# Loading, scaling and transposing a scan's B, C and D once per layer instead of once per quarter of its groups

## The chip, the cores and the metric

The kernel runs on one core of one Trainium2 chip. The metric is the device time of one execution in microseconds (us), the median over several runs. In the views of the profile PE is TensorE (its matmuls), PEld its weight loads, DVE is VectorE, ACT is ScalarE, POOL is GpSimd and SP is SyncE. ACTq stands for a DMA that ACT issues: it takes up ACT's own instruction stream.

## What is computed

One inference step of a two-layer trunk on 512 latent tokens and 128 context tokens, width 1024, fp32. Each layer: a modulated RMS norm, one input projection whose columns feed three mixers (a state-space scan, latent attention, a gated chunk mixer), a merge and an output projection; then a second norm and a convolutional feed-forward block (FFN). The change touches the parameters of the scan alone:

```python
def ssm_direction(u, h0, a_re, a_im, b_re, b_im, c_re, c_im, log_dt, reverse):
    A = lax.complex(a_re, a_im)            # 16 groups, 64 states
    Bm = lax.complex(b_re, b_im)           # (16, 64, 16 channels)
    Cm = lax.complex(c_re, c_im)           # (16, 16, 64)
    a_bar = jnp.exp(A * jnp.exp(log_dt)[:, None])
    b_bar = ((a_bar - 1.0) / A)[..., None] * Bm
    bu = jnp.einsum('gpc,blgc->blgp', b_bar, u)
    ...
    _, h = lax.associative_scan(_scan_combine, (a, bu), axis=1, reverse=reverse)
    return jnp.einsum('gcp,blgp->blgc', Cm, h).real, h_final
y = y_forward + y_backward + ssm_d * u
```

Both directions, both layers. B and C depend on the layer and the direction, not on the tokens.

## The kernel before

The tokens lie transposed in SBUF, with the channels on the partitions. Layer 0 opens with 16 loads of `w_mod` (512 KB each, on SP's queue) for the modulation, and then normalises the tokens in two halves, `norm_apply` L347: per slice of 128 channels DVE forms `nt` (L353), ACT casts it to `hh` (L357), and DVE takes the rest `hl` (L358). PE's projections need both. The weights of the input projection come through SP too and are split by ACT (`wth`, L117) and DVE (`wtl`, L118).

The scan runs in blocks of 8 tokens, so that almost all of its work is matmuls against tables: `WEd` (into a block's states), `Qd` (out of them), `Wd` (the taps inside a block) and `Td` (the rotations from block to block). `ssm_tables` (L530) makes the first three for a quarter of the groups, four of the 16, as two pairs on the two halves of the partitions, and writes them to DRAM. `ssm_load` (L683) brings them back for `ssm_quarter`. Per quarter it

- loads B in eight pieces (L547), C in eight (L551) and D in four (L626), all issued by ACT;
- transposes C on PE, and ACT copies it to `CT` (L557);
- scales B by `f = (a_bar - 1) / A` to `bb`: 12 operations of 128x32 (L91 to L96);
- and for each direction raises `bb` by the powers of a_bar (`G`, six operations of 128x256), transposes that on PE (`we`, L147) and writes `WEd`; does the same with C (`tm`, `Q`: four operations of 128x288 and four of 64x288, L607 to L611) and writes `Qd`; and last multiplies the two for the taps (PE, L632 to L635).

In layer 0 quarters 0, 1 and 2 are made by DVE, quarter 3 and the rotations (`ssm_rotations`, L648, whose fourth of four parts is the last) by POOL, all while the projection runs. The first load of the scans is `T` from `Td` (L692, on POOL's queue); its buffer has held quarter 3's `Q` before. Layer 1's four quarters are made by POOL during layer 0's FFN, one as each of the first four chunks of the FFN is written (`hooks` in `run`). `pre` is a pool open only in the opening.

The order of the instructions on each engine is not the program's: a scheduler with a model of time sorts them by priority and readiness, and each engine then works through its own list in that order.

Of the kernel before, what the change touches and what calls it, by code (L numbers as in the profile page):

```python
# [47 lines left out]
class Trunk:  # L48
# [480 lines left out]

    def ssm_tables(self, l, q, pool, E, tags={}, ps_of=None):  # L530
# [10 lines left out]
        B = t("B", [128, 2, 2, 2, 16])  # L541
        Cr = t("Cr", [128, 128])
        for d in range(2):
            for h in range(2):
                g = h * 8 + 2 * q
                for ri, nm in enumerate(("re", "im")):
                    nc.scalar.dma_start(  # L547
                        out=B[h * 64:(h + 1) * 64, ri, d],
                        in_=I["ssm_b_" + nm][l, d, g:g + 2].rearrange("g p c -> p g c"))
                    r = (ri * 2 + d) * 32  # L550
                    nc.scalar.dma_start(  # L551
                        out=Cr[r:r + 32, h * 64:(h + 1) * 64],
                        in_=I["ssm_c_" + nm][l, d, g:g + 2].rearrange("g c p -> (g c) p"))
        ps = ps_of("ct")
        self.tr(ps[:, :128], Cr)
        CT = t("CT", [128, 2, 2, 2, 16])
        nc.scalar.copy(CT.rearrange("p a b c d -> p (a b c d)"), ps[:, :128])  # L557
        bb = t("bb", [128, 2, 2, 2, 16])
        tm = [t(f"tm{i}", [128, 2 * 9 * 16]) for i in range(2)]
        for d in range(2):  # L560
            sh = [128, 2, 16]
            cs = slice(c0 + 8 * d, c0 + 8 * d + 2)
            self.complex_mul(E, bb[:, 0, d], bb[:, 1, d], B[:, 0, d], B[:, 1, d],
                             bc(self.f[:, 0, cs, None], sh), bc(self.f[:, 1, cs, None], sh),
                             [x[:, :32].rearrange("p (a b) -> p a b", b=16) for x in tm])
# [3 lines left out]
        for ri in range(2):  # L569
            for h in range(2):  # L570
                nc.scalar.copy(
                    bs[ri * 64:(ri + 1) * 64, :128].rearrange("p (d h n) -> p d h n", d=2, h=2)[:, :, h],
                    bb[h * 64:(h + 1) * 64, ri].rearrange("p d g c -> p d (g c)"))
        Qs = []
        for d in range(2):
# [6 lines left out]
            def v4(a, n):  # L582
# [7 lines left out]
                             bc(bb[:, 0, d][:, :, None, :], shp), bc(bb[:, 1, d][:, :, None, :], shp),  # L590
# [11 lines left out]
            c_re = bc(CT[:, 0, d][:, :, None, :], shp)  # L602
            c_im = bc(CT[:, 1, d][:, :, None, :], shp)
# [1152 lines left out]
```

## Time and profile before

| | |
|---|---|
| median of 3 runs | 1834.89 us (1831.66 to 1836.72) |
| the profiled execution's own time | 1831.83 us |
| its span, first to last instruction | 1830.0 us |
| mean granted TensorE clock | 0.961 |
| PE, DVE, ACT, POOL busy | 93%, 63%, 37%, 17% of the span |
| layer 0 up to the last matmul of the scan output's gate | 241.3 us |

The profile says which engine worked when, and for an engine that stood still, what released it. An engine's total says little here, since the stages differ: PE is the limit in the FFNs, and not in the opening of layer 0. The windows below are cut at events of the opening: 53.5 us is the first `nt` of the first half of the norm, 64.7 the end of its last `hl`, 68.7 and 94.7 the same of the second half, 147.4 the issue of the scans' first load, 241.3 the last matmul of the scan output's gate.

### The profile page before, as it was taken

What the parts mean: (1) busy time and instruction counts of PE and PEld (TensorE: products, weight loads), DVE (VectorE), ACT (ScalarE), POOL (GpSimd) and SP (SyncE); (2) the same over time, 40 slices, a digit from 0 to 9 for tenths busy, and PEclk for the clock granted to TensorE, in tenths of its full rate; (3) what the DMA queues carried; (4) which work ended last, traced back from release to release, by engine and by line L of the source; (5) the groups of instructions that cost most, each with busy time, mean ns of one, the idle gap of its engine ahead of it and who ended that gap; (6) DMA issues with size and microseconds to landing.
All of it is one profiled execution on the core that took longest, in us unless ns stands there. A gap on an engine that the chain in (4) does not pass through costs nothing.

```text
span 1830.0 us, 28203 instructions
## 1 busy us (share of the span) xinstructions
PE 1708.6 (93%) x10864; PEld 1499.7 (82%) x10864; DVE 1158.5 (63%) x2421; ACT 681.7 (37%) x1210; POOL 311.4 (17%) x738
## 2 busy tenths in 40 slices
PE   6869789998999999999999888999989999999998
PEld 2668644478889999999999785445989999999998
DVE  6887875667664546456566668475786464555554
ACT  4334444433442424224244355353344232332241
POOL 2886200000195060540000210000000000000000
PEclk8989799999999999999999888999989999999999
DMA  9265453301453523223122633430222131221221
GB/s 297 70 177 152 113 166 122 105 24 47 129 160 111 152 55 117 76 81 110 47 78 79 169 87 121 157 127 1 70 70 93 35 104 47 92 89 39 81 82 58
DMA packets 192998, 182.44 MB, mean 100 GB/s; under 512 B 33438, under 2 KB 153052, under 8 KB 192864
## 3 DMA queue, kind: packets, MB, share of 16 engines
q1 hardware_dynamic: 170160, 154.33, 27.5%
q0 software_dynamic: 8272, 23.87, 4.4%
q10 hardware_dynamic: 14432, 2.44, 0.7%
q8 instruction: 86, 1.41, 0.3%
q14 instruction: 48, 0.39, 0.1%
HBM read 161.94 MB, written 18.64 MB: 99 GB/s over the span
## 4 chain that ended last, share of the span: by engine, by line
PE 75%; DVE 10%; DMA 8%; ACT 4%; issue 2%; POOL 1%; ACTq 1%; DVEq 0%; POOLq 0%
PE up L141 11%; PE up L143 11%; PE up L142 10%; PE dn L142 5%; PE dn L143 5%; PE dn L141 5%; PE mod L261 3%; DMA raw<-w_mod 3%; PE o L1287 3%; PE wo L141 1%; PE wo L143 1%; PE wo L142 1%; DVE wlo L118 1%; DMA raw<-ffn_w_up 1%; PE s L1267 1%
## 5 line engine op out<-in xcount | busy, mean ns | idle before, releaser
L141 PE MATMUL up<-hh,whi 128*128 128x322 f32 x1408 | 436.8, 315 | 9.8 <-ACT hh L357 8.9
L142 PE MATMUL up<-hl,whi 128*128 128x322 f32 x1408 | 439.2, 313 | 1.8 <-DVE hl L358 1.8
L143 PE MATMUL up<-hh,wlo 128*128 128x322 f32 x1408 | 439.8, 314 | 0.0
L141 PEld LDWEIGHTS up<-hh,whi 128*128 128x128 f32 x1408 | 266.1, 190 | 21.8 <-issue 10.8
L142 PEld LDWEIGHTS up<-hl,whi 128*128 128x128 f32 x1408 | 268.3, 191 | 2.7 <-DVE hl L358 2.7
L143 PEld LDWEIGHTS up<-hh,wlo 128*128 128x128 f32 x1408 | 267.3, 190 | 1.0 <-issue 1.0
L118 DVE TENSOR_TENSOR wlo<-raw,whi 128x1024 fp32r<-128x1024 f32 (+1 forms) x116 | 147.4, 1272 | 155.2 <-ACT whi L117 146.5
L142 PE MATMUL dn<-glo,dh 128*128 128x322 f32 (+1 forms) x704 | 217.7, 311 | 0.0
L143 PE MATMUL dn<-gh,dl 128*128 128x322 f32 (+1 forms) x704 | 217.4, 310 | 0.0
L141 PE MATMUL dn<-gh,dh 128*128 128x322 f32 (+1 forms) x704 | 208.9, 310 | 2.3 <-DVE xT L1501 1.5
L1501 DVE SCALAR_TENSOR_TENSOR xT<-dn,mod,xT 128x320 f32<-128x320 f32 (+2 forms) x288 | 112.1, 435 | 128.2 <-PE dn L143 128.1
L117 ACT CAST whi<-raw 128x1024 fp32r<-128x1024 f32 (+1 forms) x116 | 120.6, 1041 | 157.1 <-PE up L142 63.8
L1532 ACT ACTIVATE cv<-up,prm,cw 128x321 f32<-128x321 f32 x88 | 54.1, 619 | 259.0 <-PE up L143 255.0
L143 PEld LDWEIGHTS dn<-gh,dl 128*128 128x128 f32 x704 | 132.9, 189 | 0.0
L141 PEld LDWEIGHTS dn<-gh,dh 128*128 128x128 f32 x704 | 130.4, 189 | 2.8 <-DVE xT L1501 1.8
L142 PEld LDWEIGHTS dn<-glo,dh 128*128 128x128 f32 x704 | 132.7, 188 | 0.0
L261 PE MATMUL mod<-raw,sT 128*32 128x512 f32 x384 | 89.7, 642 | 21.7 <-DMA raw<-w_mod 19.8
L1533 DVE SCALAR_TENSOR_TENSOR cv<-up,cw,cv 128x320 f32<-128x320 f32 x88 | 48.3, 549 | 74.3 <-ACT cv L1532 74.1
L118 DVE TENSOR_TENSOR dl<-raw,dh 128x1024 fp32r<-128x1024 f32 x44 | 53.9, 1224 | 38.3 <-ACT dh L117 38.2
L1250 DVE TENSOR_REDUCE nml<-mx 128x1 f32<-128x640 f32 x64 | 51.1, 819 | 28.3 <-PE mx L1248 28.2
L117 ACT CAST dh<-raw 128x1024 fp32r<-128x1024 f32 x44 | 46.1, 1048 | 50.7 <-DMA raw<-ffn_w_down 44.5
L141 PE MATMUL wo<-yh,whi 128*128 128x322 f32 (+1 forms) x192 | 60.0, 318 | 1.7 <-ACT yh L117 0.9
(472 smaller groups left out, 3367.4 us busy)
## 6 DMA issues: line engine op xcount, KB each, us to landing
raw<-w_mod SPq DMA_DIRECT2D x96, 512.0 KB, 4.3
raw<-ffn_w_up SPq DMA_DIRECT2D x88, 512.0 KB, 3.9
raw<-ffn_w_down SPq DMA_DIRECT2D x44, 512.0 KB, 3.4
raw<-w_in SPq DMA_DIRECT2D x10, 512.0 KB, 5.0
we<-WEd POOLq DMA_DIRECT2D x8, 512.0 KB, 4.4
qt<-Qd POOLq DMA_DIRECT2D x8, 512.0 KB, 5.0
raw<-w_out SPq DMA_DIRECT2D x16, 256.0 KB, 4.8
raw<-w_out SPq DMA_DIRECT2D x8, 512.0 KB, 3.4
```

Source lines behind the costliest of these rows:

```text
L117: self.nc.scalar.copy(hi, raw)
L118: self.nc.vector.tensor_tensor(lo, raw, hi.bitcast(F32), op=OP.subtract)
L141: mm(ps, wh, xh, start=start, stop=False)
L142: mm(ps, wh, xl, start=False, stop=False)
L143: mm(ps, wl, xh, start=False, stop=stop)
L261: nc.tensor.matmul(ps[c:c + 32, :], self.sT[:, k, :], rv[:, j, :], start=k < 4, stop=k >= 4)
L1250: V.tensor_reduce(nm[:, tt:tt + 1], pb[:, :, :320], axis=AX.XY, op=OP.max, negate=True)
L1267: mm(ps, kh[i][:, kc_], qh[i], start=True, stop=False)
L1287: mm(pb[i * 64:(i + 1) * 64, 0], Vt[:, kt, 2 * p + i], Ps[i][kt], start=kt == 0, stop=kt == 4)
L1501: self.nc.vector.scalar_tensor_tensor(self.xT[:, m, a:b], po[:, a - lo:b - lo], self.modcol(l, gi, m, c), self.xT[:, m, a:b], op0=OP.mult, ...
L1532: A.activation(z[:, 0:321], po[:, 0:321], AF.Identity, bias=b, scale=c1)
L1533: V.scalar_tensor_tensor(z[:, 1:321], po[:, 0:320], c0, z[:, 1:321], op0=OP.mult, op1=OP.add)
```

## The change

A new `ssm_parts` runs once per layer. It loads all of B (eight pieces of 64x8x16), C (four) and D (four), transposes C in four pieces into one bank, which ACT copies out at once, and scales B with 12 operations of 128x128. The results stay in SBUF in `home`, and `ssm_tables` reads slices of it. Layer 0's runs on DVE while `w_mod` loads, and its `home` borrows the buffer of `yA`, the scan's output, which is allocated later for that. Layer 1's runs on POOL in the first hook of the FFN. Per layer ACT issues 16 such loads where it issued 80, with the same bytes; DVE in layer 0 has 12 operations of 128x128 in place of 36 of 128x32, and POOL 12 fewer of 128x32; the bigger operations on G and Q are the same.

```diff
@@ -527,6 +527,43 @@
+    def ssm_parts(self, l, pool, home, E, tags=("B", "Cr")):
+        nc, I = self.nc, self.I
+        B = pool.tile([128, 2, 2, 8, 16], F32, name=self.uid("B"), tag=tags[0], bufs=1)
+        Cr = pool.tile([128, 2, 2, 2, 64], F32, name=self.uid("Cr"), tag=tags[1], bufs=1)
+        self.bbt, self.cct = home[0], home[1]
+        for d in range(2):
+            for ri, nm in enumerate(("re", "im")):
+                for h in range(2):
+                    nc.scalar.dma_start(
+                        out=B[h * 64:(h + 1) * 64, ri, d],
+                        in_=I["ssm_b_" + nm][l, d, h * 8:h * 8 + 8].rearrange("g p c -> p g c"))
+                nc.scalar.dma_start(
+                    out=Cr[:, ri, d],
+                    in_=I["ssm_c_" + nm][l, d].rearrange("(h g) c p -> (g c) h p", h=2))
+        self.dct = self.cp.tile([128, 4], F32, name=f"dct{l}")
+        nc.gpsimd.memset(self.dct, 0.0)
+        for gq in range(4):
+            g = gq // 2 * 8 + gq % 2
+            nc.scalar.dma_start(
+                out=self.dct[gq * 32:gq * 32 + 16],
+                in_=bass.AP(tensor=I["ssm_d"].tensor, offset=I["ssm_d"][l, g * 16:].offset,
+                            ap=[[1, 16], [32, 4]]))
+        ps = self.pa("ct")
+        for i in range(4):
+            self.tr(ps[:, i * 128:(i + 1) * 128],
+                    Cr[:, i // 2, i % 2].rearrange("p h c -> p (h c)"))
+        nc.scalar.copy(self.cct.rearrange("p a b c d -> p (a b c d)"), ps)
+        tm = [pool.tile([128, 8, 16], F32, name=self.uid("bt"), tag=f"tm{i}", bufs=1)
+              for i in range(2)]
+        for d in range(2):
+            cs = slice(l * 16 + 8 * d, l * 16 + 8 * d + 8)
+            sh = [128, 8, 16]
+            self.complex_mul(E, self.bbt[:, 0, d], self.bbt[:, 1, d], B[:, 0, d], B[:, 1, d],
+                             bc(self.f[:, 0, cs, None], sh), bc(self.f[:, 1, cs, None], sh), tm)
+
...
-        B = t("B", [128, 2, 2, 2, 16])
-        Cr = t("Cr", [128, 128])
-        for d in range(2):
-            for h in range(2):
-                g = h * 8 + 2 * q
-                for ri, nm in enumerate(("re", "im")):
-                    nc.scalar.dma_start(
-                        out=B[h * 64:(h + 1) * 64, ri, d],
-                        in_=I["ssm_b_" + nm][l, d, g:g + 2].rearrange("g p c -> p g c"))
-                    r = (ri * 2 + d) * 32
-                    nc.scalar.dma_start(
-                        out=Cr[r:r + 32, h * 64:(h + 1) * 64],
-                        in_=I["ssm_c_" + nm][l, d, g:g + 2].rearrange("g c p -> (g c) p"))
-        ps = ps_of("ct")
-        self.tr(ps[:, :128], Cr)
-        CT = t("CT", [128, 2, 2, 2, 16])
-        nc.scalar.copy(CT.rearrange("p a b c d -> p (a b c d)"), ps[:, :128])
-        bb = t("bb", [128, 2, 2, 2, 16])
+        bb, CT, dall = self.bbt, self.cct, self.dct
+        g0 = slice(2 * q, 2 * q + 2)
         tm = [t(f"tm{i}", [128, 2 * 9 * 16]) for i in range(2)]
-        for d in range(2):
-            sh = [128, 2, 16]
-            cs = slice(c0 + 8 * d, c0 + 8 * d + 2)
-            self.complex_mul(E, bb[:, 0, d], bb[:, 1, d], B[:, 0, d], B[:, 1, d],
-                             bc(self.f[:, 0, cs, None], sh), bc(self.f[:, 1, cs, None], sh),
-                             [x[:, :32].rearrange("p (a b) -> p a b", b=16) for x in tm])
...
-                    bb[h * 64:(h + 1) * 64, ri].rearrange("p d g c -> p d (g c)"))
+                    bb[h * 64:(h + 1) * 64, ri, :, g0].rearrange("p d g c -> p d (g c)"))
...
-                             bc(bb[:, 0, d][:, :, None, :], shp), bc(bb[:, 1, d][:, :, None, :], shp),
+                             bc(bb[:, 0, d, g0][:, :, None, :], shp), bc(bb[:, 1, d, g0][:, :, None, :], shp),
...
-            c_re = bc(CT[:, 0, d][:, :, None, :], shp)
-            c_im = bc(CT[:, 1, d][:, :, None, :], shp)
+            c_re = bc(CT[:, 0, d, g0][:, :, None, :], shp)
+            c_im = bc(CT[:, 1, d, g0][:, :, None, :], shp)
...
-        dcol = t("dcol", [128, 1])
-        nc.gpsimd.memset(dcol, 0.0)
...
-                g = h * 8 + 2 * q + e
-                nc.scalar.dma_start(out=dcol[gq * 32:gq * 32 + 16],
-                                    in_=I["ssm_d"][l, g * 16:(g + 1) * 16].rearrange("(c o) -> c o", o=1))
...
-        V.scalar_tensor_tensor(W[:, 112:128], self.id16, dcol, W[:, 112:128],
+        V.scalar_tensor_tensor(W[:, 112:128], self.id16, dall[:, q:q + 1], W[:, 112:128],
...
-        yA = mt("yA", [128, 2, NT])
...
-                    "B": "we", "Cr": "qt", "CT": "tp", "bb": "bbg", "bs": "bsg"}
+                    "bs": "bsg"}
...
+            yA = mt("yA", [128, 2, NT])
...
             with tc.tile_pool(name="pre", bufs=1, side="right") as pre:
                 mix = self.begin_layer(0, self.mod_blocks(0, (2, 0, 3, 1), pre))
+                home = mix[2].tile([128, 2, 2, 2, 8, 16], F32, name="home", tag="yA", bufs=1)
+                self.ssm_parts(0, pre, (home[:, 0], home[:, 1]), nc.vector)
...
+                            home = tb[0].tile([128, 2, 2, 2, 8, 16], F32, name="home1",
+                                              tag="home")
+                            self.ssm_parts(l + 1, tb[0], (home[:, 0], home[:, 1]), nc.gpsimd,
+                                           ("Tr", "Q0"))
                         self.ssm_tables(l + 1, q, tb[0], nc.gpsimd)
```

The scheduler makes another order of it, also for instructions that the diff does not name. On SP three of the `w_in` loads that stood between the `w_mod` loads now stand behind all 16 of them. Three places follow.

ACT at the first half of the norm (`modev` is the modulation's result, `hh` the norm's). Before:

```order
L267 COPY modev_575<-mod_549 128x512
L547 DMA B_963<-ssm_b_re 64x2x16
L357 ACTIVATE hh_418<-nt_585,mod_91 128x320
L357 ACTIVATE hh_418<-nt_589,mod_91 128x320
L551 DMA Cr_964<-ssm_c_re 32x64
L547 DMA B_963<-ssm_b_im 64x2x16
L551 DMA Cr_964<-ssm_c_im 32x64
L547 DMA B_963<-ssm_b_re 64x2x16
L357 ACTIVATE hh_418<-nt_593,mod_91 128x320
L551 DMA Cr_964<-ssm_c_re 32x64
L357 ACTIVATE hh_418<-nt_597,mod_91 128x320
```

Now:

```order
L586 COPY bs_1005<-home 64x2x32 x4
L117 CAST wth_871<-raw_869 128x576
L586 COPY bs_1582<-home 64x2x32 x4
L117 CAST wth_877<-raw_875 128x576
L117 CAST wth_883<-raw_881 128x576
L357 ACTIVATE hh_418<-nt_585,mod_91 128x320
L357 ACTIVATE hh_418<-nt_589,mod_91 128x320
L357 ACTIVATE hh_418<-nt_593,mod_91 128x320
L357 ACTIVATE hh_418<-nt_597,mod_91 128x320
L357 ACTIVATE hh_418<-nt_601,mod_91 128x320
```

The loads have gone from between the casts; three casts of `w_in` weights, each after its load, now stand ahead of the first `hh`.

DVE at the same place. Before:

```order
L353 SCALAR_TENSOR_TENSOR nt_585<-xT,mod_91,nbc_533 128x320
L353 SCALAR_TENSOR_TENSOR nt_589<-xT,mod_91,nbc_533 128x320
L95 TENSOR_TENSOR G_1624<-G_1624,tm_254_1604 128x256
L96 TENSOR_TENSOR G_1624<-G_1624,tm_255_1605 128x256
L240 TENSOR_REDUCE modred_582<-modt_577 128x8
L358 SCALAR_TENSOR_TENSOR hl_419<-nt_585,mod_91,hh_418 128x320
L245 TENSOR_TENSOR mod_91<-modred_582,prm_322 128x8
L358 SCALAR_TENSOR_TENSOR hl_419<-nt_589,mod_91,hh_418 128x320
L344 TENSOR_SCALAR nv_129_653<-nst_649 128x3
L353 SCALAR_TENSOR_TENSOR nt_593<-xT,mod_91,nbc_533 128x320
```

Now:

```order
L118 TENSOR_TENSOR wtl_872<-raw_869,wth_871 128x576
L353 SCALAR_TENSOR_TENSOR nt_585<-xT,mod_91,nbc_533 128x320
L353 SCALAR_TENSOR_TENSOR nt_589<-xT,mod_91,nbc_533 128x320
L622 TENSOR_TENSOR tm_247_1580<-pw,home 128x288
L623 TENSOR_TENSOR tm_248_1581<-pw,home 128x288
L240 TENSOR_REDUCE modred_582<-modt_577 128x8
L118 TENSOR_TENSOR wtl_878<-raw_875,wth_877 128x576
L118 TENSOR_TENSOR wtl_884<-raw_881,wth_883 128x576
L344 TENSOR_SCALAR nv_134_694<-nst_690 128x3
L358 SCALAR_TENSOR_TENSOR hl_419<-nt_585,mod_91,hh_418 128x320
L358 SCALAR_TENSOR_TENSOR hl_419<-nt_589,mod_91,hh_418 128x320
L626 TENSOR_TENSOR Q_253_1603<-tm_247_1580,tm_248_1581 64x288 x2
```

Two weight rests (`wtl`) and quarter 0's operations on C (L622 to L626, formerly L607 to L611) now stand between the norm's own.

POOL around the scans' first load. Before:

```order
L724 COPY E_2005<-h_117 128x4
L726 MEMSET E_2005 128x4
L733 MEMSET R_2029 128x4
L735 MEMSET R_2029 128x4
L733 MEMSET R_2029 128x4
L91 TENSOR_TENSOR Tr_1232<-Tr_1232,rho 128x4x8
L93 TENSOR_TENSOR Tr_1232<-Tr_1232,rho 128x4x8
L735 MEMSET R_2029 128x4
L92 TENSOR_TENSOR tr_1233<-Tr_1232,rho 128x32
L94 TENSOR_TENSOR tr_1233<-Tr_1232,rho 128x32
L95 TENSOR_TENSOR Tr_1232<-Tr_1232,tr_1233 128x4x8
L692 DMA T_1999<-Td_287 128x656
```

Now:

```order
L632 DMA Qd_282<-Q_197_1052 128x2x128 x2
L734 COPY E_1881<-h_117 128x4
L736 MEMSET E_1881 128x4
L743 MEMSET R_1905 128x4
L745 MEMSET R_1905 128x4
L743 MEMSET R_1905 128x4
L745 MEMSET R_1905 128x4
L656 DMA Wd_298<-we_1080 16x8x128 x4
L666 MEMSET Tr_1231 128x4
L667 MEMSET Tr_1231 128x4
L702 DMA T_1875<-Td_287 128x656
L91 TENSOR_TENSOR Tr_1231<-Tr_1231,rho 128x4
```

The load, formerly L692 and now L702, stood near the end of the rotations' fourth part (`Tr_1232`); now it stands ahead of that part (`Tr_1231`), which follows it.

## Rows read from the trace of the kernel before

**Rows 1.** Page, part 1: busy time, share, instructions of each engine.

```profile
PE 1708.6 (93%) x10864; PEld 1499.7 (82%) x10864; DVE 1158.5 (63%) x2421; ACT 681.7 (37%) x1210; POOL 311.4 (17%) x738
```

**Rows 2.** Busy time by engine in stretches (start:end, length, then the columns named).

```profile
core 0: us, PE busy (x) PEld busy (x) DVE busy (x) ACT busy (x) POOL busy (x), PEclk, DMA share, GB/s
...
40.00:50.00 10.00, 8.40 (x36) 2.08 (x32) 9.49 (x58) 1.75 (x3) 0.00 (x0) 0.87 0.98 345
...
53.50:64.70 11.20, 9.71 (x57) 9.13 (x58) 10.95 (x34) 5.38 (x11) 11.20 (x42) 0.85 0.11 13
64.70:68.70 4.00, 4.00 (x31) 4.00 (x30) 0.72 (x2) 0.38 (x1) 4.00 (x12) 1.00 0.07 9
68.70:94.70 26.00, 22.75 (x152) 19.39 (x152) 23.93 (x67) 10.40 (x30) 24.23 (x73) 0.93 0.31 90
94.70:125.00 30.30, 25.61 (x183) 24.32 (x182) 25.85 (x51) 11.02 (x37) 27.21 (x57) 0.89 0.61 158
125.00:147.40 22.40, 12.56 (x126) 9.43 (x122) 19.12 (x42) 10.12 (x24) 16.65 (x39) 0.77 0.74 205
147.40:241.30 93.90, 78.91 (x519) 69.08 (x518) 75.18 (x188) 44.52 (x87) 32.43 (x89) 0.87 0.39 107
```

**Rows 3.** Chain of waits, opening of layer 0: start, length, what.

```profile
55.32 1.95 DMA B<-ssm_b_im
...
66.94 1.34 ACTq L547
68.32 0.73 ACT uT L878
...
147.43 0.59 POOL T L692
```

**Rows 4.** Busy time of the rotations' instructions alone: stretch, length, POOL, PEclk, DMA, GB/s.

```profile
125.00:147.40 22.40, 7.08 (x19) 0.77 0.74 205
```

**Rows 5.** PE groups, 440 to 640 us (FFN of layer 0): busy, mean ns, idle before, releaser.

```profile
L141 PE MATMUL dn<-gh,dh 128*128 128x320 f32 (+1 forms) x88 | 25.9, 312 | 2.3 <-DVE xT L1501 1.5 <-ACT gh L117 0.8
```

**Rows 6.** Chain of waits inside layer 0's FFN.

```profile
497.18 1.97 DMA B<-ssm_b_im
```

**Rows 7.** Waits, 40 to 250 us: who waited for what, total, times, longest.

```profile
ACT uT L878 <- DMA B<-ssm_b_re: 4.7, 1, 4.7
...
ACT hh L357 <- DMA B<-ssm_b_im: 4.5, 3, 1.7
...
DVE nt L353 <- PE nbc L371: 3.3, 1, 3.3
...
POOL T L692 <- PE tap L635: 2.6, 1, 2.6
```

**Rows 8.** DVE in order of time, 48 to 53.5 us: start, length, operation.

```profile
49.17 0.28 DVE L92 TENSOR_TENSOR cm<-pw 128x128 f32<-128x128 f32 x1
49.37 0.28 DVE L93 TENSOR_TENSOR pw<-pw 128x128 f32<-128x128 f32 x1
...
51.03 0.18 DVE L95 TENSOR_TENSOR bb<-bb,tm 128x32 f32<-128x32 f32 x1
51.13 0.18 DVE L96 TENSOR_TENSOR bb<-bb,tm 128x32 f32<-128x32 f32 x1
```

**Rows 9.** DVE groups, 53.5 to 152.5 us: busy, mean ns, idle before.

```profile
L611 DVE TENSOR_TENSOR Q<-tm,tm 64x288 f32<-64x288 f32 x24 | 13.8, 575 | 0.6
L608 DVE TENSOR_TENSOR tm<-pw,CT 128x288 f32<-128x288 f32 x12 | 7.2, 600 | 0.0
```

**Rows 10.** Input and GpSimd operations of the tables: duration ns min/median/max.

```profile
L547 ACTq DMA_DIRECT2D B<-ssm_b_re x32: 602/603/762, 2.7 to 670.0; - x32
...
L91 POOL TENSOR_TENSOR bb<-B,sf x10: 230/234/240, 59.8 to 739.8; 128x32 f32<-128x32 f32 x10
...
L91 POOL TENSOR_TENSOR G<-pw,bb x10: 635/644/1235, 65.0 to 799.6; 128x256 f32<-128x256 f32 x10
```

**Rows 11.** DMA queues, 0 to 55 us: packets, MB, share of 16 engines.

```profile
q10 hardware_dynamic: 2352, 0.22, 3.3%
```

More of the change, by code (lines that the diff above doesn't have):

```diff
@@ L933, in scans @@
             self.ssm_states(l, st)
+            yA = mt("yA", [128, 2, NT])
             self.ssm_output(l, ssm, yA)
+            return yA
         if l > 0:
-            scans(tables)
+            yA = scans(tables)
         for tt in range(2, 5):
@@ L955, in mixers @@
             self.params(1)
-            scans(None)
+            yA = scans(None)
         vt = late.enter_context(tc.tile_pool(name=f"vt{l}", bufs=1, side=sa))
```

## Prediction

> **What bounds the kernel now.** I read the totals first. PE is busy 93% of the span and POOL 17% [rows 1], so work saved on POOL or ACT is worth nothing by itself; the question is where PE stands still because of the tables. The stretches of the opening show that [rows 2]: between 125 and 147.4 us PE works 12.56 of 22.4 us, while DVE works 19.12 and, before it, 25.85 of 30.3. Until 94.7 us DVE is all but full as well (10.95 of 11.2, 23.93 of 26.0). So the opening of layer 0 hangs on DVE, with POOL close behind (27.21 of 30.3).
>
> The chain of waits then shows what the tables' inputs do there [rows 3]: pieces of B, 1.95 us each, and their issues on ACT lie on the path, and the scans' first load, `T` on POOL, is a link at 147.43. In the list of waits ACT's `hh` was held by B issues for 4.5 us and `uT` for 4.7, and `T` itself by quarter 3's taps on PE for 2.6 [rows 7]. An issue costs ACT 0.60 us [rows 10], and for the first norm half they stand between the casts.
>
> In the FFN it is otherwise. The down projection's matmuls stood still 2.3 us in all of layer 0's FFN [rows 5], although a piece of B is in the chain there too [rows 6].
>
> **The change, part by part,** against the profiled execution (1831.8 us; 3.1 below the median).
>
> *Ahead of the norm (to 53.5 us).* DVE gets 12 operations of 128x128. Two such follow each other at 0.20 us, two of 128x32 at 0.10 [rows 8]: +2.4, and quarter 0's own twelve go, -1.2. Two G operations move in and two `wtl` out, about even. Net +1. On the DMA engines, 98% busy in this stretch [rows 2], more short packets come early: B has 64-byte rows, the layer's B, C and D are 5376 packets (4096, 1024, 256), and ACT's queue moved 2352 in the first 55 us before [rows 11], so some 3020 more. That queue's share gives 0.033 x 55 x 16 / 2352 = 12.3 ns for a packet on one engine, 3020 x 12.3 / 16 = 2.3 us. Against it three `w_in` loads (0.885 MB, 2.6 us at the row's 345 GB/s) now stand behind the last `w_mod`. So the modulation arrives when it did, ±0.3. The `w_in` loads land some 2.6 us after it, and their casts now head ACT's list ahead of the first `hh`; the last of them should just be through by 54, which is the thinnest cover in this sum. Behind them wait all `hh`, behind these `hl` and the projection.
>
> The Trainium skill speaks against this part: "DMA: Bandwidth & Descriptors", Specifications, asks for transfers of 512 bytes or more, since below that the engine reads, modifies and writes. If a 64-byte row therefore cost what one of 512 bytes does at 345 GB/s, 24 ns, the term would be an estimated 4.5 us. The row's 12.3 ns is no more than half of that, and I keep 2.3.
>
> *First half of the norm.* DVE takes over quarter 0's first direction of C, four `tm` and four `Q` at 0.60 and 0.58 us in the neighbourhood of POOL's work [rows 9], less where they run undisturbed: +3.4 to +4.7, and two `wtl`, +1.4. The last `hl` then comes about 5 us later, at 70 instead of 64.7. But from 64.7 to 68.7 DVE did 0.72 us of work [rows 2] and waited 3.3 us for PE's broadcast [rows 7]; that gap is filled with what came earlier. With the waits of `hh` for issues gone I put the start of the second half 3 us later.
>
> *Second half.* Six of the larger operations more (some 2.7 us), 12 of 128x32 fewer, each 0.2 us beside POOL (2.4). No change: it ends 3 us later, at 98.
>
> *From there to the scans' first load (94.7 to 147.4).* Here the change pays. Of the 54 operations on G and C that stand in this stretch, 16 have moved ahead (2 before the norm, 8 and 6 in its halves): 16 x 0.55 = -8.8. The last twelve `bb` go, -2.4. DVE stood still 7.7 of the 52.7 us [rows 2]; I give back half, the waits for B, for the copy of C and for ACT's issues: -4. With the 3 us of delay DVE's tables end 12 us earlier. POOL must follow, since it issues the load: it loses 12 `bb` of 0.23 us [rows 10], 2.8; the rotations' fourth part, 7.08 us of its time between 125 and 147.4 [rows 4], now stands behind the load; and of 8.8 us idle in these two stretches a few go. That makes -10 to -13. I take **-11** for the load: at about 136 instead of 147.4. What is late next is that fourth part, which the last quarter of the scans needs.
>
> *To the end of the opening (241.3).* PE works 78.91 and DVE 75.18 of 93.9 us there [rows 2]. The same work starts 11 us earlier, beside projections that do not. Bounds: all of it arrives (with 2 us more, from waits that shrink: -13), or little does (-2), when PE's and DVE's other work only fills in. PE's load of 84% leaves room, so I take -9.
>
> *Layer 1's tables, on POOL in the FFN.* 12 operations of 128x128, between the 0.23 us of 128x32 and the 0.64 of 128x256 [rows 10], against 48 at 0.23: POOL saves some 6 us that nobody waits for. ACT sheds 64 issues of 0.44 to 0.60 us, spread over four chunks. The PE idle of 2.3 us [rows 5] bounds the gain, zero the loss: **-1**.
>
> Sum: -9 - 1 = -10, 1821.8 on the profiled execution's scale, **1825** on the median's.
>
> **Rivals.**
> 1. *More comes through.* DVE's and POOL's saving arrives in full and its waits go too: -13.7, and the FFN gives its 2.3: -16, 1819. For it: PE has 15 us to spare after 147.4. Against it: the tables are not all that the scans wait for.
> 2. *Nothing arrives.* The load is earlier, but the scans are then held by the projection's weights and by DVE, which works 80% of that stretch: at most -2 remains, 1833. For it: DVE is full on both sides of the load. Against it: what DVE had to do there is not more than before.
> 3. *The first norm half becomes the path.* Short rows cost 24 ns (a 512-byte row at the rate of rows 2), so the last `w_in` lands 2 us later than I have it, all `hh` wait behind the casts (+2); DVE's 5 us ahead of the last `hl` are not covered, because PE's broadcast follows `hl`; and the load of `T` stays tied to quarter 3's taps on PE, as in rows 7, so that DVE's saving ends in that wait (+1 of the first part, +2, +5, and -2 from ACT's issues): +6, 1841. It decides if the last `hl` of the first half comes later than 72 us and `T` not before 146. The Trainium skill's rule of 512 bytes is its first link; this kernel's 12.3 ns speaks against it.
>
> That the change does nothing can be left out: the order shows that issues, small operations and the load of `T` have moved.
>
> **How the numbers follow.** Some 0.3% (5.5 us) is what a measurement of this kernel can tell from no change. The forecast (-6 to -14) has 0.50; rival 1 has 0.20, rival 2 0.19, rival 3 0.11. Faster is the forecast and rival 1, 0.70. The range: below, rival 1 with 5 us for waits I count only in part, 1814; above, it takes in rival 2 and the near side of rival 3, 1839. The forecast's own range is 1821 to 1829.
>
> **What would show it.** No B or C issue between the `hh`; last `hl` of the first half near 70, of the second near 98; DVE's last Q near 130; `T` issued at 134 to 138; the scan's output gate over at 232; the FFN within 2 us. The prediction is wrong if the first `hh` waits for a `w_in` cast past 56, or if `T` is early and the gate is not.

## The result and the profile after

The changed kernel takes **1860.61 us** (median; 1858.44 to 1868.61), the kernel before, on the same chip, 1834.22 us: a ratio of 1.0143, 95% interval 1.0114 to 1.0172. It is 26 us slower, where 1825 and a range up to 1839 were forecast. The profiled execution took 1868.61 us (span 1866.6), 8 us above its median, so its later stretches look some us worse than a typical run's: after_pz below, whose order is the same up to the FFN, has its gate at 258.0.

The totals hardly moved: PE does the same matmuls, POOL 54 instructions fewer [rows 1].

```profile
PE 1722.9 (92%) x10864; PEld 1509.6 (81%) x10864; DVE 1154.1 (62%) x2397; ACT 680.0 (36%) x1204; POOL 318.9 (17%) x684
```

Busy time by engine, cut at the events at which [rows 2] are cut: first `nt` 64.2 (53.5 before), first half's last `hl` 84.8 (64.7), second half 90.9 to 116.6 (68.7 to 94.7), the scans' first load 153.5 (147.4), the scan output's gate 263.3 (241.3).

```profile
core 0: us, PE busy (x) PEld busy (x) DVE busy (x) ACT busy (x) POOL busy (x), PEclk, DMA share, GB/s
40.00:50.00 10.00, 8.36 (x28) 2.94 (x28) 4.75 (x20) 4.77 (x9) 0.00 (x0) 0.53 0.64 160
64.20:84.80 20.60, 13.56 (x49) 11.73 (x50) 20.43 (x41) 4.83 (x10) 20.21 (x39) 0.50 0.23 64
84.80:90.90 6.10, 6.10 (x38) 6.10 (x38) 1.01 (x5) 0.74 (x1) 6.10 (x22) 0.82 0.01 3
90.90:116.60 25.70, 21.65 (x157) 19.22 (x157) 24.19 (x64) 10.29 (x29) 21.94 (x63) 0.95 0.38 118
116.60:153.50 36.90, 34.99 (x311) 32.66 (x311) 31.30 (x58) 17.41 (x49) 31.61 (x70) 0.89 0.74 206
153.50:263.30 109.80, 84.92 (x495) 71.36 (x493) 82.13 (x202) 45.01 (x91) 39.88 (x110) 0.78 0.33 94
```

The stretch between the second half and the load shrank from 52.7 us to 36.9: the tables do need less of DVE there. But everything ahead of it grew by 22 us, and what follows, 93.9 us before, took 109.8.

*Ahead of the norm.* ACT in order of time (start, length, operation; in brackets the idle time before it and what ended it):

```profile
24.80 0.60 ACTq L540 DMA_DIRECT2D B<-ssm_b_im  x1
27.05 0.39 ACTq L543 DMA_DIRECT2D Cr<-ssm_c_im  x1
27.48 0.47 ACT L331 ACTIVATE nsq<-xT 128x320 f32<-128x320 f32 x1 [5.03 <-DMA B<-ssm_b_re]
29.31 3.85 ACTq L540 DMA_DIRECT2D B<-ssm_b_re  x2
35.34 0.38 ACTq L543 DMA_DIRECT2D Cr<-ssm_c_re  x1
36.98 3.81 ACTq L540 DMA_DIRECT2D B<-ssm_b_im  x2
40.84 0.59 ACT L267 COPY modev<-mod 128x512 f32<-128x512 f32 x1 [12.88 <-DMA Cr<-ssm_c_re]
```

Before, ACT's first `modev` came at 31.64:

```profile
31.64 0.58 ACT L267 COPY modev<-mod 128x512 f32<-128x512 f32 x1 [0.84 <-PE mod L261]
```

ACT issues the loads in its own stream, and the issues are spread. The chain of waits of this stretch (15 to 50 us) says by what:

```profile
17.87 6.90 DMA B<-ssm_b_re
24.80 10.52 DMA B<-ssm_b_im
35.34 8.53 DMA Cr<-ssm_c_re
```

The B issued at 17.87 landed 6.90 us later, and then the one at 24.80 went out; that one landed after 10.52, and then C at 35.34. In the trace each issue names the semaphore that it waits for, and it is the one that its own landing will signal. The twelve loads of B and C have four of them (100, 111, 113, 115) in turn, so from the fifth on each waits until the load four places before it has landed. `modev`, the copy of the modulation, stands behind them: ACT was idle 12.88 us before it, though the PE work that it copies was done at 32.9. Then `w_mod`'s loads go out late too. One waits 3.3 us for PE, and the next 5.1 us for the landing of a `dct` load of ACT's that has the same semaphore (111). The DMA engines, 98% busy between 40 and 50 us before [rows 2], are 64% busy now. In the kernel before, the first B was issued at 2.7 us [rows 10], before `w_mod` filled the engines.

*In the first half of the norm* DVE is as full as before (20.43 of 20.6 us), with more to do:

```profile
L358 DVE SCALAR_TENSOR_TENSOR hl<-nt,mod,hh 128x320 fp32r<-128x320 f32 x8 | 5.0, 650 | 0.0
L353 DVE SCALAR_TENSOR_TENSOR nt<-xT,mod,nbc 128x320 f32<-128x320 f32 x8 | 4.0, 536 | 0.0
L118 DVE TENSOR_TENSOR wtl<-raw,wth 128x576 fp32r<-128x576 f32 x3 | 3.0, 1039 | 0.0
L626 DVE TENSOR_TENSOR Q<-tm,tm 64x288 f32<-64x288 f32 x4 | 2.4, 612 | 0.1
L623 DVE TENSOR_TENSOR tm<-pw,home 128x288 f32<-128x288 f32 x2 | 1.9, 974 | 0.0
```

The norm's own 16 operations cost what they did. New are `wtl`, `Q`, two kinds of `tm` on C and two on G, some 10 us, in part at twice the shortest duration (`tm` 0.97 us in the mean of two, 0.44 for the shortest of that form here).

*At the scans.* In order of time on POOL and DVE, first the fourth part of the rotations, then the first `hq`; before, that `hq` came at 173.31:

```profile
183.90 1.15 POOL L678 DMA_DIRECT2D Td<-Tr  x2 [0.30 <-POOL Tr L96]
...
187.40 0.32 DVE L771 TENSOR_TENSOR hq<-m 64x164 f32<-64x164 f32 x1 [3.36 <-DMA Td<-Tr]
```

*PE's waits up to the gate* (who, for what: total, times, longest), before from 40 us, then now from 30 us:

```profile
PE we L147 <- DVE G L95: 12.1, 3, 8.8
PE q L1055 <- ACT hsq L1061: 3.4, 1, 3.4
...
PE win L142 <- DVE hl L358: 2.0, 2, 1.2
PE glu L824 <- ACT gl L819: 1.7, 1, 1.7
PE modt L147 <- ACT modev L267: 1.5, 1, 1.5
```

```profile
PE modt L147 <- ACT modev L267: 10.7, 3, 8.5
PE wtok L911 <- DVE hl L358: 6.9, 4, 2.9
PE win L141 <- ACT sqk L998: 6.9, 1, 6.9
PE glu L834 <- ACT gl L829: 6.0, 2, 5.5
PE nbc L371 <- DVE dg L368: 4.1, 1, 4.1
PE kt L147 <- DVE ks L1177: 3.9, 1, 3.9
```

PE's 12.1 us of waiting for the tables' `G` are gone: that is what the change was expected to take away. In their place stand waits for the modulation and the norm in the opening, and for ACT and DVE in the attention and at the gate.

*In layer 0's FFN.* Waits of 440 to 680 us, two rows, and PE between the first two chunks' down projections:

```profile
ACT home L558 <- PE ct L147: 17.9, 1, 17.9
...
PE tap L642 <- POOL Q L626: 5.1, 1, 5.1
```

```profile
585.50:665.50 80.00, 71.58 (x465) 63.81 (x463) 35.68 (x54) 28.32 (x42) 35.17 (x48) 0.94 0.42 129
```

The same stretch before:

```profile
562.20:630.10 67.90, 67.90 (x461) 60.69 (x460) 35.76 (x54) 27.87 (x41) 14.24 (x29) 1.00 0.49 146
```

Of the 12.1 us more PE stands still 8.4, and its work takes 3.7 longer, at a granted clock of 0.94. From one `dn` start to the next it is now 109.2 us instead of 99.8.

### The profile page after: what moved, and what is told of

It is laid out like the page before. It is cut to its first block, busy times and chain, and to the rows that moved or that the text cites. A ratio compares the mean times of both kernels' runs of the same rounds, so it can differ in the third digit from the quotient of the medians.

```text
span 1866.6 us, 27949 instructions
## 1 busy us (share of the span) xinstructions
PE 1722.9 (92%) x10864; PEld 1509.6 (81%) x10864; DVE 1154.1 (62%) x2397; ACT 680.0 (36%) x1204; POOL 318.9 (17%) x684
## 4 chain that ended last, share of the span: by engine, by line
PE 74%; DVE 10%; DMA 8%; ACT 3%; POOL 2%; issue 2%; SPq 0%; ACTq 0%; DVEq 0%; POOLq 0%
PE up L141 11%; PE up L143 11%; PE up L142 11%; PE dn L142 5%; PE dn L143 5%; PE dn L141 5%; PE mod L261 3%; PE o L1298 2%; DMA raw<-w_mod 2%; PE wo L141 1%; PE wo L143 1%; PE wo L142 1%; PE s L1278 1%; DMA raw<-ffn_w_up 1%; PE mx L1259 1%
## 5 line engine op out<-in xcount | busy, mean ns | idle before, releaser
L118 DVE TENSOR_TENSOR wlo<-raw,whi 128x1024 fp32r<-128x1024 f32 (+1 forms) x116 | 142.3, 1228 | 152.5 <-ACT whi L117 146.0
L1543 ACT ACTIVATE cv<-up,prm,cw 128x321 f32<-128x321 f32 x88 | 54.2, 619 | 248.9 <-PE up L143 248.7
L261 PE MATMUL mod<-raw,sT 128*32 128x512 f32 x384 | 91.8, 673 | 17.8 <-DMA raw<-w_mod 17.6
L1544 DVE SCALAR_TENSOR_TENSOR cv<-up,cw,cv 128x320 f32<-128x320 f32 x88 | 48.3, 550 | 67.6 <-ACT cv L1543 66.8
L117 ACT CAST dh<-raw 128x1024 fp32r<-128x1024 f32 x44 | 46.1, 1048 | 53.8 <-DMA raw<-ffn_w_down 47.6
```

Source lines behind the costliest of these rows:

```text
L117: self.nc.scalar.copy(hi, raw)
L118: self.nc.vector.tensor_tensor(lo, raw, hi.bitcast(F32), op=OP.subtract)
L261: nc.tensor.matmul(ps[c:c + 32, :], self.sT[:, k, :], rv[:, j, :], start=k < 4, stop=k >= 4)
L1543: A.activation(z[:, 0:321], po[:, 0:321], AF.Identity, bias=b, scale=c1)
L1544: V.scalar_tensor_tensor(z[:, 1:321], po[:, 0:320], c0, z[:, 1:321], op0=OP.mult, op1=OP.add)
```

## Experiments

Each row is a ratio to the kernel before on the same chip, with its 95% interval. The last five columns are from the one profile of each (us): first `nt`, last `hl` of the first half, first load of `T`, first `hq`, end of the gate. Before, l1_clean and l1_pz have the same order up to the FFN and differ by 2.4 us at the first `nt` and 5.6 at the gate, so less than that tells nothing.

| run | ratio | nt | hl | T | hq | gate |
|---|---|---|---|---|---|---|
| before | 1 | 53.5 | 64.7 | 147.4 | 173.3 | 241.3 |
| the change | 1.0143 (1.0114 to 1.0172) | 64.2 | 84.8 | 153.5 | 187.4 | 263.3 |
| l1_only | 1.0126 (1.0085 to 1.0167) | 56.4 | 68.8 | 146.2 | 182.0 | 256.3 |
| l0_only | 1.0065 (1.0045 to 1.0085) | 63.9 | 84.5 | 151.8 | 185.5 | 256.4 |
| l1_clean | 1.0045 (1.0023 to 1.0067) | 51.8 | 62.7 | 146.4 | 174.3 | 246.1 |
| l1_pz | 1.0003 (0.9982 to 1.0024) | 54.2 | 65.2 | 149.2 | 177.3 | 246.9 |
| after_pz | 1.0082 (1.0061 to 1.0103) | 65.2 | 85.9 | 153.8 | 186.3 | 258.0 |
| early | 1.0147 (1.0119 to 1.0176) | 55.0 | 86.2 | 171.6 | 197.1 | 269.0 |
| pool_queue | 1.0186 (1.0147 to 1.0224) | 63.8 | 81.7 | 177.4 | 201.2 | 279.4 |
| l0_poolq | 1.0092 (1.0058 to 1.0127) | 55.7 | 73.4 | 164.7 | 186.8 | 268.2 |
| loads_only | 1.0087 (1.0060 to 1.0114) | 60.9 | 75.3 | 159.2 | 180.4 | 260.0 |
| l0_noload | 1.0087 (1.0061 to 1.0113) | 49.7 | 68.1 | 158.1 | 180.6 | 259.2 |
| l0_late | 1.0057 (1.0034 to 1.0080) | 55.3 | 67.6 | 146.9 | 181.6 | 258.0 |
| after_hq | 1.0134 (1.0107 to 1.0161) | 70.1 | 84.9 | 164.0 | 180.8 | 265.2 |
| before_hq | 1.0005 (0.9987 to 1.0022) | 52.1 | 64.6 | 146.8 | 157.9 | 243.9 |
| late_hq | 1.0044 (1.0025 to 1.0062) | 53.9 | 66.9 | 144.5 | 166.2 | 257.5 |
| best | 1.0069 (1.0048 to 1.0090) | 55.9 | 68.9 | 146.1 | 166.4 | 256.3 |
| late_pz | 1.0044 (1.0025 to 1.0062) | 54.9 | 67.9 | 146.4 | 175.4 | 255.9 |
| best_pz | 1.0058 (1.0035 to 1.0080) | 54.3 | 67.3 | 146.2 | 167.8 | 248.9 |
| q3_old | 1.0065 (1.0040 to 1.0089) | 55.5 | 68.2 | 155.6 | 181.0 | 256.6 |

### The two layers apart

l1_only: the old `ssm_tables` is kept as `ssm_tables_q` and used in layer 0; layer 1 uses the new one. l0_only is the reverse.

```diff
-                        self.ssm_tables(l + 1, q, tb[0], nc.gpsimd)
+                        self.ssm_tables_q(l + 1, q, tb[0], nc.gpsimd)
```

> Layer 0 loads and scales per quarter as in the kernel before, layer 1 once per layer as in the changed one. Theory A (the opening loses because ACT's early loads of B, C and D hold up ACT itself, each until an earlier one has landed; the FFN loses on its own, by layer 1's tables on POOL being late for PE): first nt of the norm at 53 to 54 us, the opening as before, a PE idle stretch of some 8 us in layer 0's FFN, in all 1839 to 1845. Rival (the FFN's loss only follows from the opening's): 1830 to 1837.

> Layer 0 once per layer, layer 1 per quarter. Theory A: first nt at 62 to 66 us as in the changed kernel, no idle stretch in the FFN, 1850 to 1856. Rival (the FFN's loss follows from the opening's): 1858 to 1864.

l0_only takes half of the loss, without a loss in the FFN. l1_only missed: its gate too came 15 us late, though layer 0's tables were the old ones. `dct` of layer 1, in a pool open from the start, let its four loads rise into the opening (31.0 to 33.9 us), `yA` was allocated later, and the order there was another. l1_clean takes both back, so which of the two made that order is not shown; its order is the old one up to the FFN.

```diff
-        self.dct = self.cp.tile([128, 4], F32, name=f"dct{l}")
+        self.dct = pool.tile([128, 4], F32, name=f"dct{l}")
```

> As l1_only, but D of layer 1 in the FFN's own pool and yA where it was, so that every engine's order up to the FFN is that of the kernel before. Theory D (layer 1's tables cost PE time in the FFN by themselves): opening as before (gate over at 239 to 244 us), then PE still in the FFN, 8 to 10 us lost between the first and the second down projection, 1841 to 1846. Rival E (l1_only's 23 us are the FFN's and the rest of the layer's): 1852 to 1860.

l1_pz then changes the bank of the four transposes of C, and after_pz does so in the changed kernel, for layer 1 alone:

```diff
-        ps = self.pa("ct")
+        ps = self.pz("ct")
```

> As l1_clean, with the one bank for the transposes of C taken from the pool of two that the quarters used before, and not from the six that the FFN's projections turn through. Theory F (in the FFN these transposes wait behind the projections for a bank, and ACT's copy and POOL's operations on C with them): the copy of C some 40 us earlier, no wait of the taps for POOL's Q, 1832 to 1838. Rival G (POOL is late because B borrows the rotations' buffer): loss stays, 1841 to 1846.

> The changed kernel with one word changed: layer 1's transposes of C go to a bank that the FFN's up and down projections don't use (layer 0's stay). Every engine's order is that of the changed kernel up to layer 0's FFN. Theory F (the FFN's part of the loss is the wait for that bank, and it adds to layer 0's part): from the down projection of the first chunk to that of the second 100 to 105 us instead of 109.2, PE no longer stands still 8 us there, 1850 to 1857 us, so layer 0 alone keeps 14 to 20. Rival (in the changed kernel the FFN would lose its 9 us anyway, because GpSimd starts layer 1's work late): 109 us again, 1858 to 1864 us.

l1_clean shows the FFN's loss by itself (17.6 us of ACT's `home` for `ct`); with the other bank the kernel is back at the time of before, within 0.2%. PE in the stretch between the two down projections, in l1_clean and then in l1_pz:

```profile
562.80:642.90 80.10, 72.45 (x466) 64.04 (x464) 35.88 (x54) 28.34 (x42) 35.29 (x48) 0.91 0.42 129
```

```profile
564.70:639.60 74.90, 69.38 (x460) 61.50 (x460) 35.22 (x54) 27.73 (x41) 33.51 (x48) 0.98 0.48 147
```

From one `dn` to the next it is 109.0 us in l1_clean and still 104.3 in l1_pz, so the bank is about half of what that stretch lost; the rest, 4.5 us, is about what the interval of its ratio leaves room for (up to 1.0024). In the changed kernel the same word gives back 10 us (1850.45; 102.8 us between the two `dn`). So the 26 us are some 10 in the FFN and some 15 in layer 0. Taken apart, l0_only's 12 us and l1_clean's 8 make only 20; the change has layer 1's four `dct` loads in the opening besides.

### The loads of the opening

early issues the 16 loads before all else; pool_queue (the changed kernel) and l0_poolq (l0_only) issue layer 0's on GpSimd's queue.

```diff
-                    nc.scalar.dma_start(
+                    nc.gpsimd.dma_start(
```

> The changed kernel with layer 0's loads issued by ACT first of all, into a buffer of their own, before the DMA engines are full. Theory A: ACT waits little for landings, first nt at 52 to 56 us, 1843 to 1851. Rival B: the packets still take their time from the loads of x and w_mod, first nt 2 to 4 us later than before at 56 to 58. Rival C (DVE's home operations and quarter 0's operations on C in the norm cost the time): first half of the norm still some 20 us long, against 11 before, in any of these.

> The changed kernel with layer 0's 16 early loads issued by POOL, which is idle then, and not by ACT. Theory A: ACT's squares for the norm run when their data is there, first nt at 52 to 57 us, 1846 to 1852. Rival B (the 64-byte rows slow the DMA engines and with them w_mod): the same packets at the same time, first nt at 62 to 66, 1858 to 1863.

> As l0_only (layer 0 once per layer, layer 1 per quarter), with all of layer 0's loads of B, C and D issued by POOL, so that ACT issues none of them ahead of the norm; pool_queue still had D of layer 1 there, which held ACT for 11.6 us. Theory A: first nt at 54 to 58 us, 1838 to 1844. Rival B (short rows slow w_mod): first nt at 62 or later, 1847 or more.

Off ACT and out of its way the first `nt` is back at 55 to 56 (in pool_queue it isn't, since there layer 1's `dct` still held ACT, 11.6 us before one `nsq`: its first issue waits for the landing of a `w_mod` load with the same semaphore). None got faster. In early the loads of the scan's rates (`srow`) come behind them, at 16.30 instead of 0.75; PE stood still 10.1 us for these, and DVE's work on the rates then stood in the first half of the norm, which took 31.2 us. GpSimd, with the loads in its list, came 17 and 30 us late with `T`.

loads_only is the kernel before with the 16 loads added beside the old ones and their results unused (its `ssm_parts` has nothing but the loads); l0_noload is l0_only with the buffers filled by constants.

```diff
+                self.ssm_parts(0, pre, None, nc.vector)
```

> The kernel before, with the 16 loads of the change added in the opening and their results not used. Theory A: the first nt comes 6 to 12 us later (60 to 66 instead of 53.5), 1842 to 1856 us. Rival (the loads cost their issues on ACT and 2 to 3 us of the DMA engines): first nt at 54 to 57, 1834 to 1841 us.

> As l0_only (layer 0 once as in the change, layer 1 per quarter, 1847.03 us), but B, C and D of layer 0 are not loaded: the buffers are filled with constants. Theory A (ACT's issues of these loads, held until earlier loads have landed, make the norm late by 10 us): first nt at 53 to 56 instead of 63.9, first half's last hl at 70 to 76, 1833 to 1841 us. Rival (the order of DVE, ACT and PE costs it, the loads don't): first nt may be early, but the gate stays 12 us late or more, 1843 to 1850 us.

Without the loads the first `nt` came at 49.7, with them alone at 60.9. loads_only shows the same wait on ACT:

```profile
35.69 0.38 ACTq L542 DMA_DIRECT2D Cr<-ssm_c_re  x1
37.17 3.59 ACTq L539 DMA_DIRECT2D B<-ssm_b_im  x2
40.80 0.58 ACT L267 COPY modev<-mod 128x512 f32<-128x512 f32 x1 [10.94 <-DMA Cr<-ssm_c_re]
```

So the loads make the norm late, and by themselves cost as much as all of layer 0's change. But l0_noload lost as much, with the first `nt` early: its first half took 18.4 us, its second ended at 104.3, and its gate was 18 us late, the sign of its rival. The two causes are not additive.

### An opening that is repaired

l0_late calls layer 0's `ssm_parts` after the scan's input, so that the loads, the scaling and quarter 0 have a lower priority.

```diff
         U = self.ssm_input(l, ssm, uT)
         if l == 0:
+            self.ssm_parts(0, tb, (home[:, 0], home[:, 1]), V)
```

> As l0_only, with layer 0's call placed behind the projection's first columns in the program, so that the scheduler gives it less weight: the first load goes out at once, the 12 operations still ahead of the norm, but none of quarter 0's operations on C and no weight rest between the norm's. Theory H (C's early copy lets quarter 0's operations push into the norm, some 9 us): first half of the norm 11 to 13 us long, 1830 to 1838. If ACT's issues alone count (theory A), first nt stays at 60 to 64 and the half at 18 to 20: 1844 to 1850.

Both halves were repaired (67.6; the second half ended at 86.4, 8 us earlier than before), `T` was on time, and the gate still at 258. Then the rotations got a buffer of their own, since the first `hq` was released by their DMA:

```diff
-            self.ssm_rotations(0, ssm, nc.gpsimd, 4, ("hq", "ys"))
+            self.ssm_rotations(0, ssm, nc.gpsimd, 4, ("Tr0", "tr0"))
```

> The changed kernel; the rotations get a buffer of their own, where the changed kernel lends them the buffer of the scan quarters' hq. Theory J (what the scans lose is a wait for that buffer: in the changed kernel the first hq at 187.40 is released by the DMA of the rotations' fourth part, which now stands behind the scans' first load): the first hq is no longer released by that DMA and starts by about 165 to 178, the scans end 8 to 15 us sooner, 1846 to 1853 us. Rival K (the scans are late because of everything that the opening left over on DVE, ACT and PE; the buffer is only what the trace happens to name): hq moves by under 4 us, 1857 to 1864 us.

> The kernel before, with the same buffer of their own for the rotations. Theory J: there too the first hq (173.31) is released by the rotations' DMA, though little late; it starts up to 10 us sooner, 1824 to 1834 us. Rival K: the scans there wait for T, U and the tables as well, nothing gained, 1832 to 1838 us.

> As l0_late (layer 0's call placed after the scan's input, layer 1 per quarter, 1848.15 us), with a buffer of their own for the rotations. Theory J: l0_late had the first norm half and the second repaired, and lost its 14 us at hq alone (181.62, against 173.31 before); with that wait gone the first hq starts by 172, the scans end at about 241 to 250, 1832 to 1842 us. Rival K: 1845 to 1850 us.

> Layer 0's call after the scan's input, the rotations in a buffer of their own, and layer 1 once per layer with its transposes of C in a bank that the FFN's up and dn don't use. If the three losses (the opening's loads, hq's buffer, the FFN's banks) are all of the change's loss, and the 12 us less work of DVE in layer 0 come through: 1820 to 1834 us. Rival: the order that the scheduler makes of it costs what the losses gave back, 1838 to 1850 us.

The theory fell. `hq` came 15 us earlier in before_hq and late_hq, 7 in after_hq, and no gate did. The wait that the profile names, 3.36 us of it, went, and the end stayed.

late_pz and best_pz take layer 0's C to another bank as well, q3_old gives GpSimd's quarter its own loads again, so that its list is nearly the old one:

```diff
-                self.ssm_tables(0, q, ssm, nc.gpsimd, tags, lambda s: self.pb(s)[:, 0])
+                self.ssm_tables_q(0, q, ssm, nc.gpsimd, tags, lambda s: self.pb(s)[:, 0])
```

> As l0_late (layer 0's call after the scan's input, layer 1 per quarter, 1848.15 us), with the transposes of C in a bank that the projection's wtok tiles don't use. In l0_late and late_hq ACT copies them out only at about 95 (late_hq 95.19), DVE stands still 3.5 us for that copy and its operations on C start at 95.8 instead of inside the second half of the norm; its tables then end at 150 to 153, against 143.9 before. Theory M (that bank is what the repaired opening lost): operations on C from about 75, the tables end at 135 to 145, the scan's gate at 240 to 249, 1832 to 1841 us. Rival K (whatever the tables do, the scans and the attention share PE and DVE, and 15 us late is what this order costs): gate at 254 to 260, 1845 to 1850 us.

> As best (layer 0's call after the scan's input, the rotations in a buffer of their own, layer 1 once per layer with its C in another bank, 1851.57 us), with layer 0's C in that other bank too. Theory M: 1830 to 1841 us. Rival K: 1846 to 1853 us.

> As late_pz (layer 0's call after the scan's input, C in another bank, layer 1 per quarter, 1845.29 us), but quarter 3, the one that GpSimd makes, loads and scales its own B and C again as before; only DVE's quarters 0 to 2 read from home. Theory N (with home ready GpSimd makes quarter 3 first and the rotations behind it: in before its second and third rotations part are issued at 89 and 115, in late_pz at 105 and 144, in l0_noload at 109 and 156, and the scans' loads follow them): GpSimd's list is that of before again, the parts come at about 89 and 115 to 120, the gate at 241 to 249, 1830 to 1841 us. Rival K (PE's work up to the gate is the same in every version, and what stands still in this order of DVE and PE is not GpSimd's doing): gate at 252 to 260, 1843 to 1850 us.

Theories M and N fell too: the gate stayed at 256 to 257. best_pz came nearest with 248.9, which is within the spread of the old order (l1_pz 246.9); its loss is elsewhere, 5 us of it between the two `dn` (104.6 us, though its bank was free), and the rest is open.

What the others have in common is read from PE up to the gate, in before, before_hq, late_pz, q3_old and the change:

```profile
0.00:241.34 241.34, 187.58 (x1193) 150.24 (x1197) 192.11 (x560) 101.31 (x221) 127.84 (x349) 0.87 0.53 153
```

```profile
0.00:243.91 243.91, 188.89 (x1185) 149.83 (x1189) 189.90 (x550) 100.26 (x221) 130.90 (x349) 0.83 0.52 152
```

```profile
0.00:255.90 255.90, 187.91 (x1193) 151.78 (x1197) 188.63 (x533) 99.95 (x218) 126.73 (x334) 0.83 0.50 144
```

```profile
0.00:256.59 256.59, 187.67 (x1194) 152.57 (x1198) 184.92 (x537) 99.36 (x219) 130.72 (x347) 0.85 0.51 145
```

```profile
0.00:263.27 263.27, 193.94 (x1189) 156.83 (x1189) 195.84 (x546) 99.31 (x219) 134.55 (x335) 0.79 0.49 140
```

PE's work ahead of the gate is the same 1185 to 1194 matmuls, nearly all of them in every version. What differs is how long PE stands still (length less busy): 53.8 and 55.0 us in the first two, 68.0, 68.9 and 69.3 in the others. In the change its work also took 6.4 us longer, at a mean granted clock of 0.79 instead of 0.87; in after_pz, with the same order, it took 187.2 us at 0.81, so that is this execution's and not the order's. DVE's total shows the saving only in q3_old (-7) and late_pz (-3.5), not in the change (+3.7). PE has the same to do in every version, and what it waits for decides.

The traces show where the scans fall behind: at DVE's first operation on `T`, `m`. In before, before_hq and late_pz:

```profile
152.47 0.84 DVE L744 TENSOR_TENSOR m<-E,T 128x656 f32<-128x656 f32 x1 [1.32 <-POOL E L727]
```

```profile
150.91 0.84 DVE L744 TENSOR_TENSOR m<-E,T 128x656 f32<-128x656 f32 x1 [4.80 <-DMA T<-Td]
```

```profile
166.98 0.83 DVE L873 TENSOR_TENSOR m<-E,T 128x656 f32<-128x656 f32 x1
```

It is at 151.5 and 154.8 in l1_clean and l1_pz, and at 159.8 or later in every other version. In late_pz `T` had landed at 151.4. But DVE's list had the chunk mixer's `gt` and `yc` and the attention's `krg` ahead of `m`, and stood still 8.8 us on the way to them. And GpSimd copied the last piece of `E`, which `m` reads too, at 163.5, amid the rotations' fourth part, which now follows the load; in before it did so at 152.2. There `m` is 14.5 us late and the gate 14.6. In before_hq `gt` comes as late as in late_hq (152.4 and 152.9), but behind `m`, and the gate is on time.

**Open** is whether that place of `m` in the lists costs the 15 us. It fits all these traces, but no version with `home` and with `m` ahead was run, and PE's gaps lie elsewhere in each (6.9 us for `sqk` in the change and in q3_old, 7.9 us for a cached input of the attention in late_hq). `home` itself is not needed for the loss. PE stands still 61 to 82 us in the versions that have it in layer 0, and 67.6 and 69.7 in loads_only and l1_only, which don't, against 53.8 to 60.0 in before, before_hq, l1_clean and l1_pz. The order is made anew with each edit. No version here beats the kernel before; l1_pz and before_hq equal it.

## Why the prediction was wrong, by its steps

- *Ahead of the norm, "+1".* Wrong by 10: the first `nt` came 10.7 us late. The packets were priced rightly, ACT's place among them not at all. Queue 10 moved 6352 packets in the first 60 us, all of them by 55:

```profile
q10 hardware_dynamic: 6352, 0.59, 8.3%
```

  That is 0.083 x 60 x 16 / 6352 = 12.5 ns for a packet on one engine, against the forecast's 12.3 [rows 11]. That is 4000 more than before and not 3020, since the 2352 hold other loads too; at 12.5 ns they are 3.1 us instead of 2.3. The estimated 24 ns from the Trainium skill's rule of 512 bytes ("DMA: Bandwidth & Descriptors", Specifications) was rightly set aside: it does not show here. What the step left out is that an issue on ACT can stand until earlier loads have landed, and that `modev` waits behind it. "The thinnest cover", the casts ahead of the first `hh`, was not the place.
- *First half, "last `hl` about 5 us later, +3 for the second".* Mis-sized. The half took 20.6 us, not 11.2 (+9.4); l0_late, without quarter 0's operations in it, took 12.3. The operations were counted rightly, but two `wtl` together took 2.29 us beside GpSimd and `tm` up to 1.05, where [rows 9] gave a mean of 0.60. The gap before the second half was not filled: it grew from 4.0 to 6.1 us, with 5.0 of it DVE's wait for PE's broadcast, which needs the first half to have ended and stood behind projection matmuls on PE. That is rival 3's condition (last `hl` after 72, `T` not before 146), and both came true; its +6 was far too small, since its first link (+2) was sized by packets and not by ACT.
- *Second half, no longer.* Right: 25.7 us.
- *To the first load, "DVE's tables end 12 us earlier, `T` at 136".* Right in size, and no gain: against the second half's end DVE's last `Q` came 16 us sooner (49.1 us after it before, 33.0 now), but 8.8 of the forecast's 12 had only moved ahead, and what moved into the first half cost its 9.4 there. Where the operations on C stayed behind the norm, in l0_late, the last `Q` ended at 152.7, later than before (143.9).
- *To the gate, "-9".* The wrong step in kind. It took the issue of `T` as the start of the scans. `T` was on time in l0_late, late_hq, best, late_pz and best_pz, and `m`, the first to use it, came at 159.8 to 167.0 instead of 152.5 and the gate 8 to 17 us late; `hq` was 15 us early in before_hq, and the gate no earlier. The room that PE's load of 84% was read as was there (84.92 of 109.8 us now, 77%), and did not help. Why `m` comes late is open, as said above.
- *Layer 1's tables, "-1, bounds 0 and -2.3".* Wrong by 10 in the other direction. Zero was taken as the bound of the loss, since nobody waited for POOL. The four transposes of C now took a bank of those that the up and down projections use, and ACT's copy waited 17.9 us for them. With another bank 10 us came back.
- *Rivals.* The third named the right side and its signs, at 0.11; the range ended 22 us short.

## What to carry over

Before a load is moved ahead, ask what stands behind its *issue* on the issuing engine, and whether the DMA engines are full at that time: here it stood until an earlier load had landed. A load on an engine that also feeds the critical path is not free because it is small. When work is merged, look up which PSUM banks and buffers the merged piece takes and who shares them: one word gave back 10 of the 26 us. And where PE does the same work in every version, judge a step by the time that PE stands still up to the next common point, and by when the first operation on a loaded table runs, not by when its load is issued or by the wait that the profile names at one link; three repairs of named waits here moved the link and not the end.

## What was not expected of the hardware

- DMA issues whose shortest took 0.38 us held ACT 12.88 us (10.94 in loads_only) while `w_mod` loaded. The Trainium skill ("DMA: Bandwidth & Descriptors", Anatomy of one DMA) says that a wait for a semaphore is taken by the issuing sequencer before dispatch; that agrees, ACT's own work stood behind such waits. But its sentence that issuing on several engines saves a time "usually small relative to the DMA itself" (Issuing engines are not separate DMA queues) does not cover this case: with the issues on GpSimd l0_poolq's first `nt` came 8.2 us ahead of l0_only's.
- In the first half of the norm PE had a granted clock of 0.50, the 1.2 GHz level, after it had stood still 8.5 us behind `modev` in the opening and 4 us ahead of the first `nt`; before it was 0.85 [rows 2].
